# A depthwise convolution's diagonal weight tiles made in an earlier layer and kept in DRAM, and its shift divided between POOL and ACT

## The chip, the cores and the metric

One core of a Trainium2 chip. The metric is the device time of one execution in microseconds (us), lower is better. The kernel before takes 2172.09 us, the median of 3 runs (2170.27 to 2172.36).

## The reference

A decoder trunk of four layers over 512 tokens of width 1024. Every layer adds a token mixer and then an MLP (1024 to 4096 to 1024, squared ReLU) to the residual rows. Layers 0 and 3 mix by attention within a window, layer 1 by a Conformer convolution module, layer 2 by a gated linear recurrence (HGRN2). The change concerns layer 1, and layer 0's MLP as a place for its work. Cut to that:

```
def conformer_conv(h, w_pw1, b_pw1, w_dw, b_dw, ln_g, ln_b, w_pw2, b_pw2):
    u = h @ w_pw1 + b_pw1
    a, gate = jnp.split(u, 2, axis=-1)
    u = a * jax.nn.sigmoid(gate)
    up = jnp.pad(u, ((0, 0), (CONV_WIDTH - 1, 0), (0, 0)))
    c = depthwise_conv(up, w_dw) + b_dw          # width 31, causal, 1024 channels
    c = jax.nn.silu(layer_norm(c, ln_g, ln_b))
    return c @ w_pw2 + b_pw2

for i in range(DEPTH):
    h = h + mixer[i](rms_norm(h, norm_mixer[i]))
    h = h + jnp.square(jax.nn.relu(rms_norm(h, norm_mlp[i]) @ mlp_w1[i])) @ mlp_w2[i]
return rms_norm(h, final_norm)
```

## The kernel before

The residual rows stay in SBUF. Every fp32 product on TensorE (PE) is done as three passes (lines 285 to 287, in `step`) over operands split in a high and a low part. For a weight, `load` makes them: ACT casts the loaded `raw` to `wh` and VectorE (DVE) subtracts, `wl = raw - wh`, both on line 262. `prefetch` does this up to five slabs ahead of PE (`W_BUFS`). Weights are loaded by SyncE (SP); for the second MLP product, POOL adds blocks of weights by accumulating DMAs (line 217).

The order of the work comes from one clock. Every `step` of PE counts it up and calls `pump`, which goes round the generators that were given to `spawn`; a generator that yields n sleeps for n steps. So a `yield` in a generator says behind how many steps of PE its next instructions stand, and each engine then runs its own list strictly in order.

An MLP (`mlp`) has four groups of 1024 hidden columns. Each begins with a first product, `linear` over four slabs of 256 columns (10.9 us each), whose results ACT turns to `us` (lines 563, 564); then come seven products of a Strassen-like scheme, whose operands `uh` and `ul` are made from `us` on lines 557 and 558 and whose results DVE adds to the rows (line 604).

Layer 1 (`conformer`) has eight blocks of 128 channels, "channel 0" to "channel 7". The pointwise product gives for each channel a gate and then a value; `glu` fetches the two from PSUM on line 930, ACT applies the sigmoid (line 933), and DVE makes the gated value on line 939. Channels 0 to 2 are convolved on DVE by `on_dve`: 30 taps each (line 893), then the subtraction of a shift (lines 881, 904). `PACE` is the least number of steps between two taps while the pointwise product lasts.

Channels 3 to 7 are convolved on PE by `on_pe`. ACT spreads the gated value over the partitions in 16 small copies (line 912); PE multiplies it with diagonal weight tiles, four groups of 9 matmuls (line 833); ACT copies the results back, four copies a group (line 919); DVE adds the bias and subtracts the shift in one instruction (line 922). The diagonal tiles, `w` of 128 x 1088, are made by DVE from the `taps` and a small identity `i4` (line 823). `Convolution.prepare` makes the first ten of the 20 while layer 1 begins, and each group's end makes one more (`build`).

`sums(j)` squares the channel on ACT (line 863) and adds channel and square to the running sums `acc1` and `acc2`, on POOL, and on DVE for the last but one (lines 868, 869). `most` then sums these over the channels with small matmuls (line 401); the last channel's sums follow at the end and are added to them in `both` (line 954). The LayerNorm's mean and root come from `both`, and with them the second pointwise product begins. The sums over the channels and the spreading of mean and root (line 391) stand on PE's list.

## Time and profile before

| | |
|---|---|
| median of 3 runs | 2172.09 us (2170.27 to 2172.36) |
| profiled execution, its own time | 2173.08 us |
| its span | 2171.3 us |
| mean granted clock of PE | 0.992 |
| busy: PE | 2121.1 us (98%) |
| busy: DVE | 1402.4 us (65%) |
| busy: ACT | 1156.5 us (53%) |
| busy: POOL | 200.5 us (9%) |
| DMA, mean over the span | 121 GB/s |

The span is the time from the first to the last instruction that the profiler saw. PE works nearly all of it. Layer 0's MLP has its first products at 167 to 211 us and again every 83 us or so; layer 1's pointwise product and convolution take 484 to 656 us, and its second pointwise product begins at 669 us.

### The profile page before, as it was taken

What the parts mean: (1) busy time and instruction counts of PE and PEld (TensorE: products, weight loads), DVE (VectorE), ACT (ScalarE), POOL (GpSimd) and SP (SyncE); (2) the same over time, 40 slices, a digit from 0 to 9 for tenths busy, and PEclk for the clock granted to TensorE, in tenths of its full rate; (3) what the DMA queues carried; (4) which work ended last, traced back from release to release, by engine and by line L of the source; (5) the groups of instructions that cost most, each with busy time, mean ns of one, the idle gap of its engine ahead of it and who ended that gap; (6) DMA issues with size and microseconds to landing.
All of it is one profiled execution on the core that took longest, in us unless ns stands there. A gap on an engine that the chain in (4) does not pass through costs nothing.

```text
span 2171.3 us, 27234 instructions
## 1 busy us (share of the span) xinstructions
PE 2121.1 (98%) x10226; PEld 1748.1 (81%) x10226; DVE 1402.4 (65%) x2226; ACT 1156.5 (53%) x2015; POOL 200.5 (9%) x193
## 2 busy tenths in 40 slices
PE   8999999999988999999999999999999999999997
PEld 7778888888877888888788888888887878888886
DVE  6864663769986375475888874547548784637547
ACT  6855454454684445445555554534536684534534
POOL 0000110110020011011300000101100000101100
PEclk9999999999998999999999999999999999999999
DMA  5154755745214375674222226567564116557553
GB/s 152 47 155 110 181 129 152 184 68 136 69 40 136 98 184 114 168 175 88 88 62 75 78 69 179 113 164 177 118 161 88 59 50 194 120 152 188 114 125 78
DMA packets 211063, 262.56 MB, mean 121 GB/s; under 512 B 9027, under 2 KB 136003, under 8 KB 210932
## 3 DMA queue, kind: packets, MB, share of 16 engines
q1 hardware_dynamic: 175540, 191.61, 28.1%
q0 software_dynamic: 35392, 69.21, 20.1%
q8 instruction: 81, 1.33, 0.2%
q14 instruction: 50, 0.41, 0.1%
HBM read 258.69 MB, written 2.10 MB: 120 GB/s over the span
## 4 chain that ended last, share of the span: by engine, by line
PE 72%; DVE 14%; ACT 5%; DMA 5%; issue 4%; SPq 0%; DVEq 0%; ACTq 0%
PE mm L285 21%; PE mm L286 21%; PE mm L287 21%; DVE wl L262 5%; DMA raw<-in_mlp_w_dram 4%; DVE rows L604 3%; PE aux L754 2%; DVE ul L558 2%; DVE uc L893 1%; PE aux L704 1%; ACT wh L262 1%; PE aux L1068 1%; ACT uc L912 1%; PE aux L438 1%; PE aux L738 1%
## 5 line engine op out<-in xcount | busy, mean ns | idle before, releaser
L262 DVE TENSOR_TENSOR wl<-raw,wh 128x1024 fp32r<-128x1024 f32 x452 | 551.2, 1220 | 538.9 <-ACT wh L262 536.3
L262 ACT CAST wh<-raw 128x1024 fp32r<-128x1024 f32 x452 | 470.0, 1048 | 497.7 <-PE mm L286 187.9
L285 PE MATMUL mm<-x,wh 128*128 128x512 f32 x1568 | 628.9, 401 | 0.0
L286 PE MATMUL mm<-x,wh 128*128 128x512 f32 x1568 | 613.7, 391 | 0.0
L287 PE MATMUL mm<-x,wl 128*128 128x512 f32 x1568 | 613.6, 391 | 0.0
L287 PEld LDWEIGHTS mm<-x,wl 128*128 128x128 f32 x1568 | 294.6, 188 | 62.5 <-issue 1.2
L286 PEld LDWEIGHTS mm<-x,wh 128*128 128x128 f32 x1568 | 295.6, 189 | 56.6 <-issue 1.8
L285 PEld LDWEIGHTS mm<-x,wh 128*128 128x128 f32 x1568 | 295.5, 188 | 55.7 <-issue 1.1
L285 PE MATMUL mm<-wh,uh 128*128 128x512 f32 x768 | 303.1, 395 | 15.9 <-DVE rows L604 12.6
L217 POOL DMA_DIRECT2D raw<-in_mlp_w_dram x128 | 153.5, 1206 | 1773.2 <-DVE wl L262 928.4
L286 PE MATMUL mm<-wl,uh 128*128 128x512 f32 x768 | 300.0, 391 | 0.0
L287 PE MATMUL mm<-wh,ul 128*128 128x512 f32 x768 | 298.0, 391 | 0.0
L285 PEld LDWEIGHTS mm<-wh,uh 128*128 128x128 f32 x768 | 144.5, 188 | 53.8 <-issue 10.6
L287 PEld LDWEIGHTS mm<-wh,ul 128*128 128x128 f32 x768 | 144.6, 188 | 30.3
L286 PEld LDWEIGHTS mm<-wl,uh 128*128 128x128 f32 x768 | 144.8, 189 | 28.9
L563 ACT ACTIVATE relu<-mm 128x512 f32<-128x512 f32 x128 | 76.0, 594 | 166.7 <-PE mm L287 166.7
L558 DVE TENSOR_TENSOR ul<-us,uh 128x1024 fp32r<-128x1024 f32 x64 | 78.0, 1218 | 32.5 <-ACT uh L557 32.5
L604 DVE SCALAR_TENSOR_TENSOR rows<-mm,nr,rows 128x512 f32<-128x512 f32 x128 | 94.9, 741 | 0.0
L564 ACT ACTIVATE us<-relu 128x512 f32<-128x512 f32 x128 | 80.9, 632 | 3.9
L285 PE MATMUL mm<-wh,y 128*128 128x512 f32 x192 | 78.1, 407 | 1.4 <-ACT y L366 1.4
L426 ACT ACTIVATE sq<-rows 128x512 f32<-128x512 f32 x64 | 40.2, 628 | 68.3 <-DVE rows L338 54.3
L287 PE MATMUL mm<-wh,y 128*128 128x512 f32 x192 | 76.0, 399 | 0.0
(232 smaller groups left out, 2546.5 us busy)
## 6 DMA issues: line engine op xcount, KB each, us to landing
raw<-in_mlp_w_dram SPq DMA_DIRECT2D x256, 512.0 KB
raw<-in_mlp_w_dram POOLq DMA_DIRECT2D x128, 512.0 KB, 6.1
raw<-in_hgrn_w_qfig_dram SPq DMA_DIRECT2D x64, 256.0 KB
raw<-in_attn_w_qkv_dram SPq DMA_DIRECT2D x20, 512.0 KB
raw<-in_attn_w_o_dram SPq DMA_DIRECT2D x16, 512.0 KB
raw<-in_conv_w_pw_dram SPq DMA_DIRECT2D x32, 256.0 KB
raw<-in_conv_w_pw_dram SPq DMA_DIRECT2D x8, 512.0 KB
raw<-in_hgrn_w_o_dram SPq DMA_DIRECT2D x8, 512.0 KB
```

Source lines behind the costliest of these rows:

```text
L217: gp.dma_start(out=wide(to), in_=block(w, r, c, h), accum_op=ALU.add)
L262: return sc.copy(wh, raw), ve.tensor_tensor(wl, raw, wh.bitcast(F32), ALU.subtract)
L285: pe.matmul(ps, sh, mh, start=start, stop=False, skip_group_check=again)
L286: pe.matmul(ps, sh, ml, start=False, stop=False, skip_group_check=again)
L287: pe.matmul(ps, sl, mh, start=False, stop=stop, skip_group_check=again)
L426: sc.activation(scratch("sq"), rows[:, b, f * T : (f + 1) * T], AF.Square, accum_out=self.ms[:, f, b : b + 1])
L438: pe.transpose(ps[:, b * P : (b + 1) * P], rows[:, b, j * P : (j + 1) * P], ident)
L558: ve.tensor_tensor(flat[1], src, flat[0].bitcast(F32), ALU.subtract)
L563: sc.activation(s, ps, AF.Relu)
L564: sc.activation(us[j // KH][:, :, j % KH, :], s.rearrange("p (h t) -> p h t", h=2), AF.Square)
L604: ve.scalar_tensor_tensor(o, banks[bank][p], norm.r2[sign][:, b : b + 1], o, ALU.mult, ALU.add)
L754: pe.matmul(po[h * HD : (h + 1) * HD, n * P : (n + 1) * P], vtok[:, n - 1 + b, kv * HD : (kv + 1) * HD], pT[:, b, n - n0, h, :], start=b = ...
```

## The change

The diagonal tiles are no longer made in layer 1. `Convolution` is made before the layers, and `prepare` runs beside layer 0's MLP. It makes each tile in four pieces of 10, 10, 10 and 4 taps (128 x 320 and 128 x 128), 80 in all, in a buffer of two, and SP writes each to a tile in DRAM. It issues pieces only where `beside_first` is set, that is within the first product of each group. In layer 1 `build` is then one load of 544 KB by SP into the same ring of ten tiles, and `ahead` starts the first ten with seven steps between two.

Line 922 becomes two instructions: ACT adds the bias in place (line 944 of the changed kernel), POOL subtracts the shift (line 945). `PACE` goes from 2.4 to 1.8, the first shift waits 12 steps instead of 4, and `acc1` and `acc2` have places of their own.

```diff
-PACE = 2.4
+PACE = 1.8
+    beside_first = [False]
-    def mlp(i, norm, nxt):
+    def mlp(i, norm, nxt, beside=None):
+            if beside:
+                spawn(beside(mp))
+                beside_first[0] = True
                 linear(norm.xs, 4, hidden, lead=KC - 1 if g == 0 else None)
+                beside_first[0] = False
         def __init__(self):
+            dram = ctx.enter_context(tc.tile_pool(name="dram", bufs=1, space=bass.MemoryType.DRAM))
+            self.stored = [dram.tile([P, self.TAPS, 32], F32, name=f"w{n}") for n in range(4 * CONV_ON_PE)]
-        def prepare(self):
-            yield 16
+        def prepare(self, pool):
+            yield 12
...
+            piece = 10
+            for n, stored in enumerate(self.stored):
+                for x in range(0, self.TAPS, piece):
+                    while not beside_first[0]:
+                        yield 1
+                    nx = min(piece, self.TAPS - x)
+                    w = pool.tile([P, piece, 32], F32, tag="w", name="w", bufs=2)[:, :nx, :]
+                    taps = self.taps[:, n // 4, n % 4, x : x + nx]
+                    ve.tensor_tensor(
+                        w, self.i4.unsqueeze(1).broadcast_to([P, nx, 32]), taps.unsqueeze(2).broadcast_to([P, nx, 32]), ALU.mult
+                    )
+                    nc.sync.dma_start(out=stored[:, x : x + nx, :], in_=w)
+                    yield 2 + x % 20 // piece
+        def ahead(self):
             for _ in range(self.AHEAD):
+                yield 7
                 self.build()
-                yield 3
         def build(self):
-            ve.tensor_tensor(
-                w, self.i4.unsqueeze(1).broadcast_to([P, nx, 32]), self.taps[:, n // 4, n % 4, :].unsqueeze(2).broadcast_to([P, nx, 32]), ALU.mult
-            )
+            nc.sync.dma_start(out=w, in_=self.stored[n])
         def sums(j):
-                    shared[k] = tmp.tile([P, T], F32, tag="acc", name=k, bufs=2)
+                    shared[k] = cp.tile([P, T], F32, name=k)
         def first_shift():
-            yield 4
+            yield 12
         def on_pe(j, t):
-            ve.scalar_tensor_tensor(cs[j], cs[j], vec("b_dw", j), shared["shift"], ALU.add, ALU.subtract)
+            sc.activation(cs[j], cs[j], AF.Identity, bias=vec("b_dw", j))
+            gp.tensor_tensor(cs[j], cs[j], shared["shift"], ALU.subtract)
             sums(j)
...
+    conv = Convolution()
-            conv = Convolution()
-            spawn(conv.prepare())
+            conv.open()
+            spawn(conv.ahead())
-        mlp(i, mid, norm)
+        mlp(i, mid, norm, conv.prepare if i == 0 else None)
```

Three places of the engines' lists, before and in the change. The changed kernel's lines stand a little lower: 262 is 263 there, 558 is 561, 604 is 609, 863 is 885, 868 and 869 are 890 and 891, 893 is 915, 904 is 926, 912 is 934, 919 is 941, 930 is 953, 939 is 962.

DVE in layer 0's MLP, from the end of group 0's first product, before (`wl` belongs to a weight slab, `ul` to the first operands of the second product):

```order
L262 TENSOR_TENSOR wl<-raw,wh 128x1024 x5
L558 TENSOR_TENSOR ul<-us,uh 128x1024
L262 TENSOR_TENSOR wl<-raw,wh 128x1024 x4
L558 TENSOR_TENSOR ul<-us,uh 128x1024
L543 TENSOR_TENSOR us_sum<-us 128x1024
```

and the second half of the same piece in the change, from the first `ul` on:

```order
L561 TENSOR_TENSOR ul<-us,uh 128x1024
L824 TENSOR_TENSOR w<-i_145,taps 128x128
L824 TENSOR_TENSOR w<-i_145,taps 128x320 x3
L263 TENSOR_TENSOR wl<-raw,wh 128x1024
L824 TENSOR_TENSOR w<-i_145,taps 128x128
L824 TENSOR_TENSOR w<-i_145,taps 128x320
L263 TENSOR_TENSOR wl<-raw,wh 128x1024
L824 TENSOR_TENSOR w<-i_145,taps 128x320 x2
L824 TENSOR_TENSOR w<-i_145,taps 128x128
L824 TENSOR_TENSOR w<-i_145,taps 128x320 x2
L263 TENSOR_TENSOR wl<-raw,wh 128x1024
```

Two or five builds stand between two `wl`, seven in the time of a slab, and the next `ul` stands behind them. Such builds stand also ahead of this, in the output projection of layer 0's attention, and in the first products of groups 1 and 2.

DVE at the end of layer 1's pointwise product, before, from channel 1's last tap to channel 7's gated value (line 939) and on:

```order
L893 SCALAR_TENSOR_TENSOR uc<-uc,vecT 128x511
L893 SCALAR_TENSOR_TENSOR uc<-uc,vecT 128x493
L904 TENSOR_TENSOR uc<-uc,shift 128x512
L922 SCALAR_TENSOR_TENSOR uc<-uc,vecT,shift 128x512
L262 TENSOR_TENSOR wl<-raw,wh 128x1024
L930 TENSOR_TENSOR a<-mm,r_4296 128x512
L893 SCALAR_TENSOR_TENSOR uc<-uc,vecT 128x494
L939 SCALAR_TENSOR_TENSOR a<-a,vecT,gate 128x512
L893 SCALAR_TENSOR_TENSOR uc<-uc,vecT 128x495
```

and in the change, to channel 7's gated value (line 962) and on:

```order
L915 SCALAR_TENSOR_TENSOR uc<-uc,vecT 128x510
L915 SCALAR_TENSOR_TENSOR uc<-uc,vecT 128x511
L926 TENSOR_TENSOR uc<-uc,shift 128x512
L953 TENSOR_TENSOR a<-mm,r_4580 128x512
L263 TENSOR_TENSOR wl<-raw,wh 128x1024
L953 TENSOR_TENSOR a<-mm,r_4580 128x512
L962 SCALAR_TENSOR_TENSOR a<-a,vecT,gate 128x512
L263 TENSOR_TENSOR wl<-raw,wh 128x1024
L890 TENSOR_TENSOR acc_5030<-acc_5030,uc 128x512
L891 TENSOR_TENSOR acc_5031<-acc_5031,csq 128x512
```

Before, 18 taps of channel 2 (widths 494 to 511) stood behind that value; in the change all taps stand ahead of it, and only the last running sums (`acc`) behind.

ACT from channel 5's last copies back to the squares of channel 7, before (`csq` is a square, `uc<-a` the copies out, `uc<-aux` the copies back):

```order
L863 ACTIVATE csq<-uc 128x512 x2
L262 CAST wh<-raw 128x1024
L919 COPY uc<-aux 32x128
L912 COPY uc<-a 32x128 x16
L919 COPY uc<-aux 32x128 x15
L863 ACTIVATE csq<-uc 128x512
L919 COPY uc<-aux 32x128 x16
L863 ACTIVATE csq<-uc 128x512 x2
```

and in the change:

```order
L944 ACTIVATE uc<-uc,vecT 128x512
L885 ACTIVATE csq<-uc 128x512
L263 CAST wh<-raw 128x1024
L885 ACTIVATE csq<-uc 128x512
L934 COPY uc<-a 32x128 x16
L941 COPY uc<-aux 32x128 x16
L944 ACTIVATE uc<-uc,vecT 128x512
L941 COPY uc<-aux 32x128
L885 ACTIVATE csq<-uc 128x512
L941 COPY uc<-aux 32x128 x15
L944 ACTIVATE uc<-uc,vecT 128x512
L885 ACTIVATE csq<-uc 128x512
```

Each channel of PE's has a bias (line 944) ahead of its square, and between the two stands POOL's subtraction on POOL's own list. On PE, the four matmuls that sum `acc1` stood behind all 36 of channel 7; in the change they stand behind 13 of these, and those of `acc2` three further on.

## Rows read from the trace of the kernel before

**Rows 1.** Windows of 4 us; busy us and instructions, granted clock, DMA share, GB/s; sum.

```profile
652.00:656.00 4.00, 0.06 (x1) 0.10 (x1) 3.90 (x7) 2.52 (x6) 0.00 (x0) 0.92 0.71 248
...
660.00:664.00 4.00, 3.75 (x17) 3.66 (x18) 0.49 (x4) 0.00 (x1) 0.00 (x0) 0.50 1.02 387
...
sum 48.00, PE 32.62 PEld 28.71 DVE 34.47 ACT 29.86 POOL 10.39; mean PE 2.72 PEld 2.39 DVE 2.87 ACT 2.49 POOL 0.87
```

**Rows 2.** Timeline of PE: start us, us, engine, line, operation, times, [idle before].

```profile
601.30 0.39 PE L287 MATMUL mm<-x,wl 128*128 128x512 f32 x1
...
621.22 9.48 PE L833 MATMUL aux<-uc,w 128*128 128x128 f32 x72
639.67 12.04 PE L833 MATMUL aux<-uc,w 128*128 128x128 f32 x72 [8.98 <-ACT uc L919]
655.94 3.54 PE L401 MATMUL aux<-ones_d,acc 128*128 128x1 f32 x16 [4.22 <-ACT csq L863]
```

**Rows 3.** Timeline of DVE at the end of the conformer.

```profile
605.66 1.75 DVE L893 SCALAR_TENSOR_TENSOR uc<-uc,vecT 128x502 f32<-128x502 f32 x1
...
609.02 0.74 DVE L939 SCALAR_TENSOR_TENSOR a<-a,vecT,gate 128x512 f32<-128x512 f32 x1
...
610.82 0.73 DVE L893 SCALAR_TENSOR_TENSOR uc<-uc,vecT 128x504 f32<-128x504 f32 x1
...
628.14 0.68 DVE L930 TENSOR_TENSOR a<-mm,r 128x512 f32<-128x512 f32 x1
...
629.81 1.75 DVE L939 SCALAR_TENSOR_TENSOR a<-a,vecT,gate 128x512 f32<-128x512 f32 x1
...
663.41 0.16 DVE L954 TENSOR_TENSOR both<-most,aux 128x8 f32<-128x8 f32 x1 [3.73 <-PE aux L401]
```

**Rows 4.** Timeline of ACT there.

```profile
609.79 6.95 ACT L912 COPY uc<-a 32x128 f32<-32x128 f32 x16 [4.52 <-DVE a L939]
...
628.72 0.38 ACT L919 COPY uc<-aux 32x128 f32<-32x128 f32 x1
631.59 6.84 ACT L912 COPY uc<-a 32x128 f32<-32x128 f32 x16 [2.50 <-DVE a L939]
638.45 5.87 ACT L919 COPY uc<-aux 32x128 f32<-32x128 f32 x15
...
654.56 1.29 ACT L863 ACTIVATE csq<-uc 128x512 f32<-128x512 f32 x2 [1.26 <-DVE uc L904]
```

**Rows 5.** Groups of DVE's instructions, 484 to 656: busy us, mean ns, idle before.

```profile
L823 DVE TENSOR_TENSOR w<-i,taps 128x1088 f32<-128x1088 f32 x20 | 25.4, 1280 | 0.0
...
L922 DVE SCALAR_TENSOR_TENSOR uc<-uc,vecT,shift 128x512 f32<-128x512 f32 x5 | 3.7, 745 | 8.1 <-ACT uc L919 8.1
```

**Rows 6.** Windows of two stages (columns as in rows 1).

```profile
484.00:632.00 148.00, 144.83 (x775) 120.30 (x773) 139.99 (x189) 93.87 (x180) 18.32 (x13) 1.00 0.32 86
...
250.00:294.00 44.00, 44.00 (x195) 36.44 (x195) 13.15 (x12) 17.74 (x24) 2.38 (x2) 1.00 0.56 135
```

**Rows 7.** Timeline of POOL in the conformer.

```profile
604.75 2.12 POOL L868 TENSOR_TENSOR acc<-acc,uc 128x512 f32<-128x512 f32 x1 [16.91 <-DVE uc L922]
...
623.11 1.27 POOL L868 TENSOR_TENSOR acc<-acc,uc 128x512 f32<-128x512 f32 x1 [14.55 <-DVE uc L904]
```

**Rows 8.** Timeline of SP at the kernel's end: the last write.

```profile
2167.78 0.33 SPq L511 DMA_DIRECT2D out_dram<-rows  x1
```

**Rows 9.** Waits of SP's queue: total us, times, longest.

```profile
SPq L1270 <- DMA out_dram<-rows: 1.7, 1, 1.7
```

**Rows 10.** Timeline of DVE in layer 0's MLP, first product of group 0.

```profile
198.55 1.23 DVE L262 TENSOR_TENSOR wl<-raw,wh 128x1024 fp32r<-128x1024 f32 x1 [4.69 <-ACT wh L262]
...
209.43 1.23 DVE L262 TENSOR_TENSOR wl<-raw,wh 128x1024 fp32r<-128x1024 f32 x1 [6.94 <-ACT wh L262]
...
214.39 1.23 DVE L558 TENSOR_TENSOR ul<-us,uh 128x1024 fp32r<-128x1024 f32 x1 [1.02 <-ACT uh L557]
```

**Rows 11.** Timeline of PE there: the second product.

```profile
216.99 0.39 PE L287 MATMUL aux<-wh,ul 128*128 128x512 f32 x1
```

More of the change, by code (lines that the diff above doesn't have):

```diff
@@ L793, in __init__ @@
         def __init__(self):
-            cp = self.pool = tc.tile_pool(name="cv", bufs=1)
-            self.cp = cp.__enter__()
             self.built = []
-            self.taps = self.cp.tile([P, CONV_ON_PE, 4, self.TAPS], F32, name="taps")
-            self.i4 = self.cp.tile([P, 32], F32, name="i4")
-        def close(self):
-            self.pool.__exit__(None, None, None)
-        def prepare(self):
-            yield 16
+            dram = ctx.enter_context(tc.tile_pool(name="dram", bufs=1, space=bass.MemoryType.DRAM))
+            self.stored = [dram.tile([P, self.TAPS, 32], F32, name=f"w{n}") for n in range(4 * CONV_ON_PE)]
+            self.taps = const.tile([P, CONV_ON_PE, 4, self.TAPS], F32, name="taps")
+            self.i4 = const.tile([P, 32], F32, name="i4")
+        def prepare(self, pool):
+            yield 12
             j0, r0 = KC - CONV_ON_PE, vrows["w_dw"]
@@ L807, in prepare @@
             ve.memset(self.taps, 0.0)
-            yield 2
+            yield 4
             for g in range(4):
```

12 lines of the change are left out of this document (8 added, 4 removed).

## The prediction

> **What bounds the kernel now.** I read the page first: PE is busy 98% of the span (the table above), so a change on DVE, ACT or POOL can only win where PE waits for them. The table of windows says where that is. In the 48 us from 628 to 676 PE works 32.62 us [rows 1]; it does next to nothing in 652 to 656, and its granted clock stands at 0.50, the lower of its two levels (1.2 GHz), in 660 to 664. This is the end of the conformer: the depthwise convolution of its last channel block (channel 7 below), then the LayerNorm sums. Everything the change moves out of the conformer must pay here or nowhere.
>
> Next, who was late. PE ends the last product of the pointwise projection at 621.22, where its convolution of channel 6 begins [rows 2]; DVE fetches that product only at 628.14 and hands over channel 7's gated values ("a7", line 939) at 629.81 + 1.75 = 631.56 [rows 3]; ACT begins channel 7's 16 copies at 631.59 and ends the last at 638.43 [rows 4]; PE begins channel 7's convolution at 639.67, after 8.98 us of waiting [rows 2]. Channel 6 is the same: PE ends that product at 601.69 [rows 2], and a6 is handed over at 609.02 + 0.74 = 609.76 [rows 3]. So DVE runs some 7 to 8 us behind PE. But ACT is nearly as late: from 609.79 to 628.72 + 0.38 = 629.10 it works without a gap [rows 4], 19.3 us, and then waits only 2.50 for a7. This is the point on which my forecast turns.
>
> After that the chain is PE (36 matmuls, 12.04, to 651.71), ACT's last copies, DVE's shift, the squares on ACT (654.56), 16 sum matmuls, and "both" on DVE at 663.41 [rows 2, 3, 4].
>
> **The change, part by part.** The sum is made against the profiled execution, 2173.08 us; the median of the three runs, 2172.09, is 0.99 lower.
>
> *1. The conformer up to channel 7's copies.* DVE loses 20 tile builds (25.4 us) and five shifts (3.7 us) of the 139.99 us that it works in 484 to 632 [rows 5, 6]. If a7 followed directly it would come far earlier. But the order fills the room: the taps of the three channels that DVE convolves itself, which before ran on into PE's idle time (633 to 653), now all stand ahead of a7. Between the gated values of channels 4 and 5 stood 14 taps, 4 builds and a shift, and now 24 taps; between 5 and 6, 16 taps, 4 builds and a shift, and now 21 taps and a subtraction; between 6 and 7, 14 taps, 2 builds and two shifts, and now 7 taps and one. A tap is 0.73 alone [rows 3], of which some 0.65 is its step in a row of taps (0.08 overlaps the next); a build is 1.28, a step of 1.20. So: 4 to 5, 14 x 0.65 + 4.8 + 0.67 = 14.6 against 24 x 0.65 = 15.6, +1.0; 5 to 6, 15.9 against 14.3, -1.6. That is -0.6 for a6.
>
> POOL then gives some of it back. Its subtraction is of the form of the running sums it already makes, 2.12 beside a working DVE and 1.27 when DVE rests [rows 7]. The tap at 605.66 that runs beside one takes 1.75, one at 610.82 that runs alone 0.73 [rows 3]: +1.02 to DVE. Two such subtractions (of channels 3 and 4) run before a6 is made: +2.0. a6 comes at 609.76 - 0.6 + 2.0 = 611.2.
>
> From there ACT has its own list in order: channel 6's 16 copies, 16 copies back of channel 5, gate, table load, two weight casts, one bias, two squares, then channel 7's copies. It is the 19.3 us of before, less one copy (0.38), plus a bias that I take at the 0.63 of a square (two in 1.29 [rows 4]) and a wait for POOL's subtraction between bias and square, 1.27: 20.8. Channel 7's copies start at 632.0 (before 631.59): **+0.4**. a7 itself is 7 taps, two fetches, two wl and a subtraction behind a6, some 10 us, and is not what ends last. Bounds: -6.5 (rival A), and +2 with POOL's 2.12 in place of 1.27 and a third collision.
>
> *2. The tail.* Copies of channel 7 end at 632.0 + 6.84 = 638.8; the 16 copies back of channel 6 at 645.1 (15 took 5.87 [rows 4]); bias 645.8; POOL 647.1; DVE's add 647.8. PE starts at 640.2 on channel 7. Its order now holds a sum over acc1 after 13 of the 36 matmuls, and that sum waits for this add. The lower clock makes the first ones slow: 36 took 12.04 here, but 9.48 for channel 6 (0.263 each) [rows 2]; at 0.5 us each for the 11 of the first 5.4 us, the 13 end at some 646.3, so PE is held 1.5 us. Then two groups of sum matmuls, about 1.0 each at full clock (16 rows take 3.54, or 1.8 a group, at the lower one [rows 2]), and 23 x 0.263 = 6.05: 655.9. Copies back 1.6, bias 0.63, POOL 1.27, square 0.63: 660.0. Two groups of sums remain instead of four: the first at 659.4, and with 1.8 for each "both" stands at 663.1, against 663.41. So the tail is 31.1 long instead of 31.8: **-0.7**. What was gained (two sums off the end, a DVE list that is empty) is given back by three engines in a row (ACT, POOL, ACT) where one DVE instruction of 0.74 stood. Bounds: -2.4 if the hold does not occur, +5 if it costs the clock (rival D).
>
> *3. The builds in layer 0's MLP.* 80 pieces, 320 or 128 wide; by width a wide one is about 1.28 x 320/1088 + 0.05 = 0.43. The first products leave room: in 250 to 294 DVE works 13.15 of 44.00 [rows 6], and 24 or 28 builds are 12. The two-buffer tile is the question: two more builds need two writes landed. The nearest write is the kernel's last, 512 KB: 0.33 of issue, then 1.7 of waiting [rows 8, 9], 2.0 in all. A pair of 160 KB pieces thus comes round in 0.43 + 2.0 + 0.33 for the second issue = 2.8. Seven builds stand in each slab of 10.88 us (the step between the wl rows, 198.55 to 209.43 [rows 10]), which allows 3.1 a pair. **0**, with little to spare; other end in rival B. ACT and PE see nothing of it while wl and ul keep their places: ul is made at 214.39 + 1.23 = 215.62 and first used at 216.99 [rows 10, 11], 1.4 of slack.
>
> *4. The rest.* 16 builds in attention 0's output projection, PE saturated there: **0**, at most +1. Twenty reads of 544 KB on SP: 11.1 MB at 387 GB/s [rows 1] are 29 us of DMA time in a stretch of 148 us that uses 0.32 of it [rows 6]: **0**, at most +3 should one of the loads queue behind a read that waits for its write. The changed pace and the copies of taps are in the orders above.
>
> Sum: 2173.08 + 0.4 - 0.7 = 2172.8, as a median **2171.8**: no change.
>
> **A rule against the change.** Row first: beside a POOL operation of 2.12 the tap grew by 1.02, not by 2.12 [rows 3, 7]. The Trainium skill, "SBUF — State Buffer", section "Who interferes with whom", says that a VectorE instruction with two SBUF inputs and a GpSimd instruction that reads SBUF exclude each other: whoever is first holds the shared ports for its whole instruction. By it moving a subtraction to POOL can take all of POOL's time from DVE. This trace agrees that the two collide, not that one is blocked throughout.
>
> **Rivals.**
> A, *DVE was the only late engine* (faster). Without builds DVE keeps up and fetches each product when PE ends it: a6 at 601.69 + 0.68 + 0.74, and a wl (1.21) in the way, 604.3; ACT's 20.8 gives 625.1, 6.5 before 631.59. With the tail, 2173.08 - 6.5 - 0.7 = 2165.9, median 2164.9. For it: 29 us really leave DVE, and it is DVE that ended ACT's waits. Against it: the order puts 24 and 21 taps where builds stood. 0.25.
> B, *DVE waits for the writes* (slower). If a pair's writes queue behind the loads of the same slab (135 GB/s [rows 6] x 10.88 us is 2.9 loads of 512 KB, each 1.35 us at 387 GB/s, for 3.5 pairs), a pair takes 2.8 + 0.83 x 1.35 = 3.9. It decides from 3.1 on. Over the last 13 builds ahead of ul the delay is 6.5 x 0.8 - 1.4 = 3.8, in two groups 7.6: median 2179.4. For it: the margin is 0.3 us. Against: the row of 2.0 is for three times the bytes. 0.15.
> C, *POOL holds DVE throughout*: 1.77 for 1.02 at the two subtractions ahead of a6, +1.5: 2173.3, still no change. The Trainium skill's rule named above would make it so. 0.06.
> D, *the hold keeps PE at 1.2 GHz* (slower). The 23 matmuls at 0.5 are 5.4 longer than at 0.263: median 2177.2. For it: the clock did fall after waits here [rows 1]. 0.09.
>
> **How the numbers follow.** Forecast 0.45, its own range 2168 to 2176.5 (-4 and +4.5, the bounds of parts 1, 2 and 4 together); A 0.25, B 0.15, C 0.06, D 0.09. The limit of 0.2% is 4.3 us, about what a measurement of this kernel can tell from no change: 2167.7 and 2176.4. Faster: A and 0.03 of the forecast, 0.28. Slower: B, D and 0.03, 0.27. The same: 0.45. The range takes in A and B: 2163.5 to 2180.
>
> **What would show it.** Right: ACT's copies of channel 7 start at 631 to 633 with no wait for DVE before them; the sum over acc1 begins 1 to 2 us after the matmul before it; "both" at about 663; no wait of DVE for a write in 165 to 300 that delays a wl. Wrong: copies of channel 7 at 627 or earlier (A); PE idle before a product with ul in layer 0's MLP, the conformer shifted later as a whole (B); a granted clock of 0.50 from the hold to the end of channel 7 (D).

## The result: 1.1% slower, lost in layer 0

| | before | after |
|---|---|---|
| median | 2171.64 us (4 runs, 2170.27 to 2172.36) | 2196.44 us (4 runs, 2193.01 to 2198.63) |
| ratio | | 1.0114, 95% interval 1.0096 to 1.0131 |
| span of the profiled execution | 2171.3 us | 2196.9 us |
| busy: PE, DVE, ACT, POOL | 2121.1, 1402.4, 1156.5, 200.5 | 2130.1, 1406.4, 1160.0, 206.7 |
| written to HBM | 2.10 MB | 13.24 MB |

24.8 us more, where no change was forecast (2171.8, range 2163.5 to 2180.0). The side is that of rival B, the size more than three times its price.

**Where the time went.** PE does the same 8160 weight matmuls in the same order in both. So the n-th of them in one trace can be set against the n-th in the other: its start after, less its start before. I give that "lateness" for eight places; the second row says where the matmul stands in the trace of before. The runs of the experiments are in the same table, since each of them is read from it (in seven of them some of the 8160 change places with near ones, 132 at most).

| matmul n | 336 | 480 | 672 | 1056 | 1152 | 2064 | 2304 | last |
|---|---|---|---|---|---|---|---|---|
| at, before | 142 | 178 | 222 | 311 | 333 | 547 | 682 | 2163 |
| stage | layer 0: attention, end | MLP, group 0, first product | after its first ul | group 1, after its first ul | group 1 | layer 1: pointwise product | its second one | |
| after | 2.4 | 8.5 | 13.2 | 21.7 | 20.7 | 21.7 | 23.8 | 25.4 |
| no_write | 3.7 | 3.7 | 3.7 | 2.9 | 2.6 | 2.3 | 6.0 | 3.1 |
| write_free | 2.8 | 6.6 | 6.6 | 6.0 | 6.1 | 6.4 | 8.5 | 8.4 |
| no_build | 2.8 | 2.8 | 2.8 | 2.0 | 1.8 | 1.3 | 3.7 | -0.5 |
| write_act | 2.1 | 11.3 | 17.3 | 32.3 | 31.3 | 31.7 | 35.4 | 35.1 |
| nb_late | 1.6 | 1.8 | 1.8 | 4.3 | 5.9 | 11.2 | 16.6 | 11.5 |
| spread_held | 2.0 | 2.1 | 2.1 | 9.1 | 16.6 | 26.7 | 28.7 | 29.9 |
| nb_keep | 2.7 | 2.7 | 2.7 | 1.8 | 1.5 | 2.0 | -2.4 | -4.9 |
| bufs5 | 3.1 | 6.7 | 16.1 | 15.3 | 15.3 | 15.6 | 19.2 | 20.1 |
| bufs5_keep | 1.3 | 6.1 | 15.6 | 14.1 | 14.1 | 14.4 | 7.8 | 6.9 |
| before_split | -0.3 | -0.3 | -0.3 | -0.9 | -1.1 | -1.0 | -3.0 | -2.6 |
| bk22 | -1.4 | -1.4 | -1.4 | -2.2 | -2.2 | -2.4 | 1.5 | -0.8 |
| bks22 | -0.7 | -0.7 | -0.7 | -1.5 | -1.7 | -1.6 | 0.5 | -0.1 |
| paced | 0.3 | 0.3 | 4.8 | 4.3 | 4.3 | 4.8 | 10.2 | 8.2 |
| paced_keep | 0.8 | 0.8 | 5.3 | 4.4 | 4.5 | 4.8 | -1.4 | -0.6 |
| nb_keep20 | 2.4 | 2.4 | 2.4 | 1.5 | 1.1 | 0.7 | -5.4 | -8.9 |
| paced_keep_dve | -0.2 | -0.2 | 2.4 | 3.1 | 3.6 | 4.0 | -0.3 | -1.9 |
| paced_keep_g0 | 0.6 | 0.6 | 0.7 | 1.8 | 3.1 | 6.4 | -0.3 | -1.9 |
| paced_keep_b5 | 0.5 | 0.5 | 0.5 | 0.0 | 0.0 | -0.1 | -5.8 | -4.6 |

A difference along a row is time won or lost there; one trace against another leaves about 1 us of the start. The late layers, which no edit touches, wander by up to 5 between the last two columns (no_build from 3.7 to -0.5, nb_late from 16.6 to 11.5), so the last column is no measure of an edit.

The row "after" says it at once: 2.4 in attention 0, then 6.1, 4.7 and 8.5 at three places of layer 0's MLP, 2.1 at the end of layer 1, and small change. What DVE did there, in the timeline of the changed kernel (start, length, engine, line, tile, times, and in brackets the idle time before the row and what ended it):

```profile
167.43 0.49 DVE L824 TENSOR_TENSOR w<-i,taps 128x320 f32<-128x320 f32 x1 [3.76 <-DMA w<-w]
170.50 0.29 DVE L824 TENSOR_TENSOR w<-i,taps 128x128 f32<-128x128 f32 x1 [2.57 <-DMA w<-w]
...
173.78 0.68 DVE L339 TENSOR_TENSOR rows<-rows,mm 128x512 f32<-128x512 f32 x1
...
180.21 0.69 DVE L824 TENSOR_TENSOR w<-i,taps 128x320 f32<-128x320 f32 x2 [2.22 <-DMA w<-w]
180.82 2.72 DVE L448 SCALAR_TENSOR_TENSOR x<-aux,vecT,x 128x512 fp32r<-128x512 f32 x4
...
219.24 0.49 DVE L824 TENSOR_TENSOR w<-i,taps 128x320 f32<-128x320 f32 x1 [3.79 <-DMA w<-w]
221.52 0.89 DVE L824 TENSOR_TENSOR w<-i,taps 128x128 f32<-128x128 f32 x2 [1.79 <-DMA w<-w]
...
226.03 1.22 DVE L263 TENSOR_TENSOR wl<-raw,wh 128x1024 fp32r<-128x1024 f32 x1
227.17 1.22 DVE L561 TENSOR_TENSOR ul<-us,uh 128x1024 fp32r<-128x1024 f32 x1
```

It waits for "DMA w<-w", the write of a piece two builds earlier, up to 4.4 us at a time (the table below). Behind the waits stands what PE needs next: `rows` (line 339) at 173.78, the last sum of attention 0's output projection, and at 227.17 the `ul` (line 561) with which PE's second product of group 0 begins. In [rows 10] that `ul` began at 214.39; the sum of `rows`, line 338 there, stood in the kernel before at

```profile
166.79 0.68 DVE L338 TENSOR_TENSOR rows<-rows,mm 128x512 f32<-128x512 f32 x1
```

The totals, by the table of waits (total us, times, longest):

```profile
DVE w L824 <- DMA w<-w: 73.8, 39, 4.4
```

```profile
PE aux L855 <- ACT uc L941: 10.4, 2, 9.9
PE aux L288 <- DVE ul L561: 9.3, 2, 6.6
...
PE aux L439 <- DVE rows L339: 3.8, 1, 3.8
PE aux L402 <- POOL uc L945: 3.7, 1, 3.7
```

So the first of the three losses is not in the MLP's own builds: PE waits 3.80 for `rows` at the start of the MLP, behind the builds that stand in attention 0's output projection, and only 0.2 for `x` (line 448, at 180.82). The other two are the two `ul`, 9.3 us together.

```profile
174.52 0.47 PE L439 MATMUL aux<-ident,rows 128*128 128x128 f32 x1 [3.80 <-DVE rows L339]
...
319.20 0.80 PE L288 MATMUL aux<-wh,ul 128*128 128x512 f32 x1 [6.56 <-DVE ul L561]
```

PE pays once more when it goes on: after the 6.56 its granted clock is at the lower level for a while (the table of windows, columns as in [rows 1]), and from 326 it is 1.00 again. After the 3.80 it was 0.80 and 0.77 in 172 to 180.

```profile
318.00:322.00 4.00, 2.80 (x7) 2.23 (x8) 4.00 (x6) 1.05 (x1) 1.19 (x1) 0.50 0.84 215
322.00:326.00 4.00, 4.00 (x14) 3.16 (x13) 3.40 (x5) 1.48 (x2) 1.20 (x1) 0.68 0.89 131
```

Layer 1 went much as the prediction had it up to channel 7's copies. ACT, DVE, POOL and PE there:

```profile
633.40 6.95 ACT L934 COPY uc<-a 32x128 f32<-32x128 f32 x16 [2.99 <-DVE a L962]
...
652.21 0.63 ACT L885 ACTIVATE csq<-uc 128x512 f32<-128x512 f32 x1 [1.44 <-POOL uc L945]
...
654.21 6.79 ACT L934 COPY uc<-a 32x128 f32<-32x128 f32 x16
661.01 6.21 ACT L941 COPY uc<-aux 32x128 f32<-32x128 f32 x16
```

```profile
632.63 0.74 DVE L962 SCALAR_TENSOR_TENSOR a<-a,vecT,gate 128x512 f32<-128x512 f32 x1
...
648.43 1.23 DVE L263 TENSOR_TENSOR wl<-raw,wh 128x1024 fp32r<-128x1024 f32 x1 [7.24 <-ACT wh L263]
...
650.29 0.75 DVE L962 SCALAR_TENSOR_TENSOR a<-a,vecT,gate 128x512 f32<-128x512 f32 x1
...
669.35 0.69 DVE L890 TENSOR_TENSOR acc<-acc,uc 128x512 f32<-128x512 f32 x1 [13.41 <-POOL uc L945]
...
686.86 0.16 DVE L977 TENSOR_TENSOR both<-most,aux 128x8 f32<-128x8 f32 x1 [13.88 <-PE aux L402]
```

```profile
662.60 6.85 PE L855 MATMUL aux<-uc,w 128*128 128x128 f32 x26 [9.94 <-ACT uc L941]
670.19 1.02 PE L402 MATMUL aux<-ones_d,acc 128*128 128x1 f32 x8 [0.75 <-DVE acc L890]
...
672.64 6.90 PE L855 MATMUL aux<-uc,w 128*128 128x122 f32 x40
683.25 1.87 PE L402 MATMUL aux<-ones_d,uc 128*128 128x1 f32 x8 [3.71 <-POOL uc L945]
```

Less the 21.74 by which layer 1 starts late, a6 is made at 611.6 (632.63 + 0.74) and channel 7's copies start at 632.5; a7 has been ready for three us by then (650.29 + 0.75 = 651.04 against 654.21) and ACT works without a wait for DVE between 633.40 and 654.21. The matching rows of before are [rows 3, 4].

### The profile page after: what moved, and what is told of

The parts are those of the page before. It is cut to its first block, busy times and chain, and to the rows that moved or that the text cites. A ratio compares the mean times of both kernels' runs of the same rounds, so it can differ in the third digit from the quotient of the medians.

```text
span 2196.9 us, 27550 instructions
## 1 busy us (share of the span) xinstructions
PE 2130.1 (97%) x10226; PEld 1751.6 (80%) x10226; DVE 1406.4 (64%) x2281; ACT 1160.0 (53%) x2020; POOL 206.7 (9%) x198
## 3 DMA queue, kind: packets, MB, share of 16 engines
q8 instruction: 81, 1.33, 0.2%
HBM read 269.83 MB, written 13.24 MB: 129 GB/s over the span
## 4 chain that ended last, share of the span: by engine, by line
PE 62%; DVE 16%; DMA 10%; issue 8%; ACT 4%; POOL 0%; SPq 0%; DVEq 0%; ACTq 0%; POOLq 0%
PE mm L286 18%; PE mm L287 17%; PE mm L288 17%; DVE wl L263 6%; DMA w<-w 5%; DMA raw<-in_mlp_w_dram 4%; DVE rows L609 3%; DVE ul L561 2%; PE aux L759 2%; PE aux L709 1%; DVE uc L915 1%; ACT wh L263 1%; PE aux L1091 1%; PE aux L439 1%; PE aux L743 1%
## 5 line engine op out<-in xcount | busy, mean ns | idle before, releaser
L824 DVE TENSOR_TENSOR w<-i,taps 128x320 f32<-128x320 f32 x80 | 33.8, 440 | 75.6 <-DMA w<-w 73.8
L286 PE MATMUL mm<-wh,y 128*128 128x512 f32 x192 | 78.2, 407 | 1.4 <-ACT y L367 1.4
```

Source lines behind the costliest of these rows:

```text
L286: pe.matmul(ps, sh, mh, start=start, stop=False, skip_group_check=again)
L824: ve.tensor_tensor(w, self.i4.unsqueeze(1).broadcast_to([P, nx, 32]), taps.unsqueeze(2).broadcast_to([P, nx, 32]), ALU.mult)
```

## The experiments

All are built on the changed kernel unless said otherwise. The kernel before ran beside them, at medians of 2169.4 to 2171.5; each ratio is to the runs beside it, and a difference of two runs that had different runs of before beside them is safer by the ratios.

**1. Builds without writes.**

```diff
-                    nc.sync.dma_start(out=stored[:, x : x + nx, :], in_=w)
-            nc.sync.dma_start(out=w, in_=self.stored[n])
+            nc.sync.dma_start(out=w, in_=mlp_w1[1][n % 8 * P : n % 8 * P + P, : self.TAPS * 32].rearrange(...))
```

> The 80 builds stay in DVE's list in layer 0, but they are not written to DRAM (the loads in layer 1 take other data of the same size), so no build waits for a write. Theory (the loss in layer 0's MLP, 18.3 us between the first slab of its first group and group 2, is DVE waiting for the writes of the two-buffer tile with wl, x and ul queued behind): that loss goes, and the kernel takes 2196.4 - 18.3 = about 2178, with no wait of DVE for a DMA of w. Rival 1 (the builds' own 28 us of DVE work delay wl and ul): it stays near 2196. Rival 2 (the 11 MB of writes slow the weight loads): about 2178 too, and told apart by write_free.

2173.68 us, 1.001 (1.0001 to 1.0019). The loss in layer 0's MLP is gone (3.7 from attention 0 on, and no more up to group 1). Rival 1 falls: the builds' own work costs nothing where it now stands. That is not where it stood: with no write to wait for, all 80 builds are done by 190, 44 of them before 170, while the change builds until 378. Run 13 has builds in all four groups.

**2. Writes that no build waits for.**

```diff
-                    nc.sync.dma_start(out=stored[:, x : x + nx, :], in_=w)
+                    nc.sync.dma_start(out=stored[:, x : x + nx, :], in_=self.taps.rearrange(...)[:, : 32 * nx].rearrange(...))
```

> The 80 builds and the 80 writes both stay, of the same sizes and in the same places, but each write takes its data from the table of taps instead of the tile just built, so that no build waits for a write; what is stored is not the tile. Theory (waiting): about 2178, as without writes, within 2 us. Rival 2 (DMA traffic of the writes, which share the 16 engines with the weight loads): stays at 2190 or more. In between, by so much as the traffic counts.

2182.12 us, 1.0049 (1.0034 to 1.0065). In between: 14.3 less than the change, and 8.4 over no_write, so about two thirds of the loss is waiting and the rest goes with the writes as such. In the trace 3.8 of the 8.4 fall at one place, the start of group 0, where a `wl` ahead of `x` waits for a weight that landed late; against no_write, 2.8 more come behind layer 1 (the last two columns), in layers that no edit touches, and I can't say why. The expectation was wrong in one point: the builds, as in 1, are not in the same places. Without a buffer to wait for, DVE's list has up to 17 of them in a row (5.92 us from 187.07 on), which by itself costs nothing. The split of the loss holds for writes bunched like this (timeline of write_free):

```profile
175.86 1.23 DVE L263 TENSOR_TENSOR wl<-raw,wh 128x1024 fp32r<-128x1024 f32 x1 [3.88 <-ACT wh L263]
177.00 2.72 DVE L448 SCALAR_TENSOR_TENSOR x<-aux,vecT,x 128x512 fp32r<-128x512 f32 x4
```

**3. Neither builds nor writes.**

```diff
+            return
             piece = 10
```

(and the loads as in 1)

> Neither builds nor writes in layer 0, only the 16 copies of taps; the loads in layer 1 take other data of the same size. What is left is the change in layer 1 alone. Theory: 2196.4 - 18.3 for the MLP and up to 2.4 for attention 0, so 2175.7 to 2178, that is 4 to 6 slower than the kernel before, of which 2 are the end of the conformer (both sums 1.7 later against the start of layer 1 than before) and the rest drift and layer 0's start. Rival (the conformer gains when layer 0 leaves it alone, since DMA and DVE start it undisturbed): below 2171.

2173.89 us, 1.001 (1.0001 to 1.0019): the builds are free, and the change in layer 1 with the copies of taps is 2.4 slower than before. The table has 2.8 by the end of attention 0 and 2.4 more at the end of layer 1. The first is in DVE's list: 8 and 4 copies (line 814) stand ahead of three `wl` at 40.78, which before began at 38.10, and PE waits for the last of them and for what follows (timelines of no_build).

```profile
36.68 2.07 DVE L814 COPY taps<-vecT 32x155 f32<-32x155 f32 x8
...
40.78 3.50 DVE L263 TENSOR_TENSOR wl<-raw,wh 128x1024 fp32r<-128x1024 f32 x3
```

```profile
42.06 0.50 PE L288 MATMUL mm<-x,wl 128*128 128x512 f32 x1 [0.54 <-DVE wl L263]
...
45.14 0.35 PE L709 MATMUL aux<-kh,qs 128*128 128x256 f32 x1 [1.19 <-DVE qs L693]
```

**4. The shift alone, in the kernel before.**

```diff
-            ve.scalar_tensor_tensor(cs[j], cs[j], vec("b_dw", j), shared["shift"], ALU.add, ALU.subtract)
+            sc.activation(cs[j], cs[j], AF.Identity, bias=vec("b_dw", j))
+            gp.tensor_tensor(cs[j], cs[j], shared["shift"], ALU.subtract)
```

> The kernel before, with line 922 alone made into a bias on ACT and a subtraction on POOL. Theory (ACT and POOL in a row cost more at the end than DVE's one instruction, and nothing is won before it since ACT is as late as DVE): the tail +1.2 (0.72 + 1.27 for 0.74), and channel 7's copies 0 to 2 later: 2172 to 2175. Rival (DVE is the late engine, and 3.7 us less work there bring channel 7 forward): 2168 to 2170.

2170.17 us, 0.9994 (0.9986 to 1.0003): no difference that can be told in the time; the trace has 2.0 won at the end of layer 1. That is the rival's direction, but not its path: channel 7's copies start at 633.81, later than the 631.59 before, as the theory had it. What is won lies behind them: "both" stands at 660.53, before at 663.41, so the tail that the theory made 1.2 longer is shorter. In the kernel before, the shift of channel 6 on DVE waits for ACT and holds nine taps behind it; in before_split twelve taps run on without a wait.

```profile
644.35 0.75 DVE L922 SCALAR_TENSOR_TENSOR uc<-uc,vecT,shift 128x512 f32<-128x512 f32 x1 [4.71 <-ACT uc L919]
645.02 8.78 DVE L893 SCALAR_TENSOR_TENSOR uc<-uc,vecT 128x503 f32<-128x503 f32 x9
```

```profile
635.48 9.32 DVE L893 SCALAR_TENSOR_TENSOR uc<-uc,vecT 128x500 f32<-128x500 f32 x12
```

**5. The writes issued by ACT.**

```diff
-                    nc.sync.dma_start(out=stored[:, x : x + nx, :], in_=w)
+                    nc.scalar.dma_start(out=stored[:, x : x + nx, :], in_=w)
```

> The changed kernel with the 80 writes issued by ACT instead of SP; builds, buffers and order of DVE's builds as in the change. Theory (a write waits behind the weight loads that SP has issued before it on the same 16 DMA engines, whoever issues it): the time from issue to the build that reuses the buffer stays at some 4 us (median 3.8 in the change) and the kernel at 2190 to 2198, or worse, since ACT's own list now holds issues that wait for builds. Rival (SP's own queue is the cause: its list or its ring is served in order): from issue to reuse falls to about 2, as in the quiet cases (1.6 to 1.9), and the kernel to 2182 or less.

2206.39 us, 1.0163 (1.015 to 1.0177). From a write's issue to the build that takes its buffer again the median is 3.7 us, against 3.8 in the change: SP's queue is not the cause. ACT now waits for builds, which is worse (the table of waits; the results' `relu` waits 17.4 more):

```profile
ACT wh L263 <- DVE w L824: 17.6, 7, 4.8
```

**6, 7. Copies and builds held back in the program's order.** `keep` (line 80) makes an instruction keep the program's order against others that are kept. Here it is put on the weight subtractions of layer 0 and on the copies (nb_late), and on the builds too, with no gate and `yield 5` (spread_held).

```diff
+        if held[0]:
+            keep(sub)
-            yield 12
+            while not beside_first[0]:
+                yield 1
+                    keep(ve.tensor_copy(...))
```

> As no_build (no builds and writes in layer 0, the loads in layer 1 take other data), but the 16 copies of taps are held until the first product of layer 0's MLP; to hold them, DVE's list keeps the program's order between them and the weight subtractions of layer 0. Theory (12 of these copies, 3.4 us, stood on DVE ahead of three weight subtractions in layer 0's attention, at 36.7 to 40.8, and PE came 2 to 2.4 later from there on): 2.0 to 2.4 less than no_build, 2171 to 2172, and a start of layer 0's MLP as in the kernel before. Rival (these 2 are given back within the attention): the same as no_build, 2173.9.

> The whole change again, with builds and writes, but the copies of taps as in nb_late, and the builds spread over all of layer 0's MLP, one in five steps (3.4 us), held in the program's order against the weight subtractions. Two buffers as before, so a pair has 6.8 us for its writes instead of 3.1. Theory: the waits (14.3 of the loss, change against write_free) and the copies (2.4) go, the traffic of the writes stays (8.4 or less): 2179.6, not under 2173.9. Rival (builds between the second products, where DVE is busy 33 of 39 us, delay operands): over 2185.

2184.81 us (1.0062, 1.005 to 1.0075) and 2201.41 us (1.0138, 1.0123 to 1.0154). Both missed. The copies do leave the attention (1.6 there instead of 2.8), but nb_late, which has no builds, loses some 9 us in layer 0's MLP: with the weight subtractions kept to the program's order DVE's list is worse than without. PE now waits for `wl` there (5.7 us in 150 to 560), and not once in the kernel before. So neither run speaks to its question; another way to move builds was needed (11 to 15).

**8. The gated values kept ahead of the taps**, on 3, with `PACE = 2.4`:

```diff
-            ve.scalar_tensor_tensor(u, t, vec("b_pw1", j, 0), gates[j], ALU.add, ALU.mult)
+            ins = ve.scalar_tensor_tensor(u, t, vec("b_pw1", j, 0), gates[j], ALU.add, ALU.mult)
+            if j >= ON_DVE:
+                keep(ins)
-                    ve.scalar_tensor_tensor(c[:, late:], ...)
+                    ins = ve.scalar_tensor_tensor(c[:, late:], ...)
+                    if len(us) > ON_DVE:
+                        keep(ins)
```

> As no_build, but the gated values of the channels that PE convolves keep their place in the program's order against the taps (pace 2.4): 27 taps now stand behind channel 7's value instead of none. Theory of the prediction's rival A, put to the test (DVE's taps ahead of a6 and a7 are what kept the conformer from gaining; 31 us less work on DVE then show): channel 7's copies start 4 to 7 earlier against the start of layer 1, and the kernel takes 2167 to 2170. Rival (ACT's own list of 20.8 us between channel 6's copies and channel 7's ends last, with POOL's subtraction in it): at most 2 less than no_build, 2172 to 2174.

2167.64 us, 0.9982 (0.9974 to 0.9991), 6.2 less than no_build. Channel 7's copies now start at 625.29, the time of rival A (625.1; layer 1 itself starts 1 to 2 late here). a6 is made at 603.6 (602.69 + 0.90), 8 us earlier than in the change, and ACT's list from there takes the same 20.7 (604.55 to 625.29). What ends last is now the 26 taps behind: PE waits 10.0 for DVE's running sums (timelines of nb_keep):

```profile
604.55 6.92 ACT L937 COPY uc<-a 32x128 f32<-32x128 f32 x16
...
625.29 6.93 ACT L937 COPY uc<-a 32x128 f32<-32x128 f32 x16
```

```profile
602.69 0.90 DVE L965 SCALAR_TENSOR_TENSOR a<-a,vecT,gate 128x512 f32<-128x512 f32 x1
...
628.12 23.61 DVE L916 SCALAR_TENSOR_TENSOR uc<-uc,vecT 128x486 f32<-128x486 f32 x26
```

**9, 10. Five buffers instead of two**, one buffer of summed weights less; bufs5_keep with 8 added, at a pace of 2.0.

```diff
-                group[key] = raw_tile(sumpool[0], bufs=8)
+                group[key] = raw_tile(sumpool[0], bufs=7 if n_layer[0] == 0 else 8)
-                    w = pool.tile([P, piece, 32], F32, tag="w", name="w", bufs=2)[:, :nx, :]
+                    w = pool.tile([P, piece, 32], F32, tag="w", name="w", bufs=5)[:, :nx, :]
```

> The whole change, with five buffers for the built pieces instead of two; the room comes from one of the eight buffers for summed weights in layer 0. Nothing else is changed. Theory (two buffers against a time of some 4 us from a write's issue to the reuse): five buffers at one build in 1.55 us allow 7 us, the builds no longer wait (their 74 us of waiting for a DMA of w fall under 10), and what stays is the traffic and the copies of taps: 2182 like write_free, within 3. Rival (the order of the builds in DVE's list, not the number of buffers): over 2190.

> As bufs5, and with the gated values of PE's channels kept ahead of the taps as in nb_keep, at a pace of 2.0 that leaves 15 taps behind channel 7's value. Theory (the two parts add up): bufs5 less the 6.2 that nb_keep gained over no_build, and up to 4 more since in nb_keep the 26 taps behind ended last (651.8, four us after ACT's copies): bufs5 less 6 to 10, about 2174. Rival (with the writes there the conformer starts with its loads of w behind, and keeps nothing): as bufs5.

2191.37 us (1.0101, 1.0086 to 1.0116) and 2181.91 us (1.0062, 1.0048 to 1.0076). The theory fell short: group 1 loses nothing now, but group 0 loses more at its `ul` (9.4), and the MLP's start still 3.6. By the ratios five buffers gain 2.8 over the change, and the two intervals overlap. The five buffers were filled at once. In DVE's list builds are drawn forward as far as buffers allow, it seems as if a write took no time, so ten pieces stand between two `wl` (timeline of bufs5) and the same wait is back:

```profile
202.88 1.93 DVE L825 TENSOR_TENSOR w<-i,taps 128x320 f32<-128x320 f32 x5 [1.13 <-DMA w<-w]
209.40 1.93 DVE L825 TENSOR_TENSOR w<-i,taps 128x320 f32<-128x320 f32 x5 [4.58 <-DMA w<-w]
211.24 1.22 DVE L264 TENSOR_TENSOR wl<-raw,wh 128x1024 fp32r<-128x1024 f32 x1
```

The conformer's part of bufs5_keep is as expected: 6.6 won between the two pointwise products (14.4 to 7.8), and 9.5 less than bufs5.

**11, 12. The kernel before with the gated values kept ahead**, at a pace of 2.2, as it is (bk22) and with the split shift (bks22).

> The kernel before, builds in layer 1 and shift on DVE as they were, with nothing but the gated values of PE's channels kept in the program's order against the taps (pace 2.2 instead of 2.4). Theory (the order of the taps, not the builds, decides when channel 7's copies start): 2 to 5 less than before, 2166 to 2169. Rival (with the builds on DVE it has no room, and what is taken off ahead of channel 7 comes last behind it): 2171 or more.

> As bk22, with the shift divided between ACT and POOL as in the change. Theory: before_split gained 1.3 in the median over the kernel before, since DVE is the engine with the longest list there; on top of bk22 another 0 to 2: 2164 to 2168, below both kernels. Rival (ACT's list of 20.8 between channels 6 and 7 ends last once the taps are out of the way, and the bias and the wait for POOL lengthen it): 1 to 2 above bk22.

2173.06 us (1.0019, 1.001 to 1.0028) and 2173.93 us (1.0024, 1.0014 to 1.0034). Both missed. With the builds on DVE, channel 7's copies start no earlier against layer 1's own start (629.25 + 2.4 in bk22, 633.64 + 1.6 in bks22, before 631.59), and the taps that are taken off ahead of channel 7 come last behind it: PE waits for DVE's running sums, 7.2 and 3.3. As far as these two runs at one pace show, moving the builds is needed for the gain, as the change meant it.

**13. Builds paced by a true dependence.** Two buffers, as in the change.

```diff
+                    if beside:
+                        zero = mp.tile([P, 1], F32, tag="zero", name="zero", bufs=2)
+                        sc.mul(zero, s[:, :1], 0.0)
+                        zeros.append(zero)
...
+            flat = self.taps.rearrange("p a b c -> p (a b c)")
+            ve.tensor_scalar(flat, flat, zeros[0], None, ALU.add)
...
+                i4 = pool.tile([P, 32], F32, tag="i4e", name="i4e", bufs=1)
+                ve.tensor_scalar(i4, self.i4, zeros[e], None, ALU.add)
+                for _ in range((3, 2)[e % 2]):
```

> The whole change with two buffers, but the builds and the copies of taps get a true dependence on the first product's results: after each 128-column result ACT makes a zero from it, DVE adds it to the small identity, and the next three or two builds use that. So at most three builds stand between two weight subtractions (five in 10.9 us instead of seven, over all four groups), and none nor the copies of taps in layer 0's attention. Theory (the list packs builds ahead of wl, x and ul, since it is made without the time of the writes; two buffers then hold up what stands behind): the waits and the attention's 2 us go, the writes' traffic stays: 2171 + 8.4 at most + conformer 2.5, so 2174 to 2180, and five buffers are not needed. Rival (a build that waits stalls PE wherever it stands): over 2185.

2178.88 us, 1.0039 (1.0026 to 1.0051). The same 80 builds and writes with the same two buffers, 17.6 less than the change (16 by the ratios): where and how densely they stand decides. The run doesn't tell apart the bounded packing, the lower rate, the four groups instead of three and the empty attention. Attention 0 loses nothing, and in layer 0's MLP one place is left, `ul` of group 0 (4.5). But the end of layer 1 loses 5.4, where the change lost 2.1 with the same code: PE's hold at `acc1` was 1.86 here, the clock behind it the lower one, and channel 7's last 20 matmuls took 7.98 (columns as in [rows 1]).

```profile
656.00:660.00 4.00, 4.00 (x19) 3.54 (x18) 0.17 (x1) 0.83 (x3) 0.00 (x0) 0.50 0.00 0
660.00:664.00 4.00, 4.00 (x19) 3.68 (x18) 0.00 (x0) 1.21 (x4) 0.00 (x0) 0.55 0.00 0
```

**14. The same with 8.**

> As paced, with the gated values of PE's channels kept ahead of the taps (pace 2.0, 15 taps behind channel 7's value). Theory: the conformer gains 6.0 against the start of layer 1, as bufs5_keep showed, instead of losing 2.5: paced less 8 or 9, 2166 to 2172, at or below the kernel before. Rival: the writes' traffic takes it all, 2174 or more.

2170.79 us, 1.0003 (0.9994 to 1.0011): level with the kernel before; 4.5 lost in layer 0, 6.2 won at the end of layer 1.

**15. The bound: 8 at a pace of 2.0, without builds.**

> As nb_keep (no builds and no writes in layer 0, other data loaded in layer 1), at a pace of 2.0, which leaves 15 taps instead of 27 behind channel 7's value. It bounds what the conformer's part can give when layer 0 costs nothing. Theory: in nb_keep the taps behind ended last, some 4 us after ACT's copies, so 2 to 4 below it: 2164 to 2166. Rival (more taps ahead hold channels 6 and 7 up by as much): the same as nb_keep, 2167.6.

2162.56 us, 0.9965 (0.9951 to 0.9978), 5.1 under nb_keep (4.0 when each is set against before beside it). This leaves out the builds; it is what layer 1 gives with these lists.

**16. Bias and shift on DVE again, on 14.**

> As paced_keep, with bias and shift again one instruction on DVE. Theory (with DVE relieved, ACT's list between channels 6 and 7 ends last; the bias and the wait for POOL's subtraction are 2 us of it, and the tail's three engines in a row another 1.2): 1 to 3 below paced_keep. Rival (DVE's instruction waits in its list behind taps): the same or above.

2172.52 us, 1.0007 (0.9999 to 1.0016): not below 14, and the two intervals overlap. The split earns a little or nothing here as well.

**17, 18. The place that is left.** On 14: no builds at group 0's last two results and more later (paced_keep_g0), or five buffers as in 9 (paced_keep_b5).

> As paced_keep, with no builds at the last two results of group 0 and three instead of two at some results of the later groups. In paced_keep the one loss left in layer 0 was 4.5 us at ul of group 0, where the last three builds of that group stood just ahead of it behind a wait of 5.1 for a write. Theory: that goes, and the kernel takes 2170.8 - 4.5 = 2166 to 2167, below the kernel before. Rival (three builds at a result bring the same wait to the later groups): 2169 or more.

> As paced_keep, with five buffers for the pieces (one buffer for summed weights less in layer 0). With the packing bounded, buffers should now do what they did not do in bufs5: no build waits for a write ahead of ul. Theory: the loss at ul of group 0 goes, 2166 to 2167, and the builds' waits for w fall from 37 us to under 10. Rival (the loss is the traffic, weights that come late, and no matter of buffers): 2170 or more.

2171.21 us (1.0005, 0.9996 to 1.0014) and **2166.82 us (0.9984, 0.9975 to 0.9993)**. Moving three builds only moved the wait: the later groups now lose 5.7 together (0.7 to 6.4). Five buffers with bounded packing remove it. Up to layer 1 this kernel is within 0.5 of before everywhere, with 80 builds and 11 MB of writes in it, and no wait of DVE for a write is left (the table of waits of paced_keep_b5, 160 to 480; `i4e` are the waits for ACT's zeros):

```profile
DVE i4e L831 <- ACT zero L572: 47.4, 14, 4.5
DVE wl L265 <- ACT wh L265: 45.4, 39, 3.9
```

So up to layer 1 the writes' traffic costs nothing that shows when they are spread over four groups; bunched, in write_free, it cost some 4 in layer 0. Against 15, which has neither builds nor writes, this kernel is level at the second pointwise product (-5.8 and -5.4) and yet 4.3 slower in all; these 4 fall in later layers, where PE waits 11.1 for `rows` and 7.3 in 15, and no run here says why. This kernel beats both: the one before by 3.4, the change by some 28 (by the ratios).

## Why the prediction was wrong, point by point

- **The step that failed: part 3**, "a pair of 160 KB pieces thus comes round in 0.43 + 2.0 + 0.33", 2.8, within the 3.1 that the list allows. The 2.0 of the kernel's last write holds where little else moves. In the change a write takes from its issue to the reuse of its buffer 3.8 us in the median. The 18 shortest took 1.6 to 2.1, with a DMA share of 0.14 to 0.49 meanwhile; of the 33 that took 3.8 to 7.4 all but one had 0.60 or more. The write that I took [rows 8, 9] had no load beside it; the stretch to be priced has a DMA share of 0.56 [rows 6]. The term was 0 and measured 18.3 (2.4 to 20.7 in the table), in it 6.1 that began in part 4's output projection.
- **Rival B** had the mechanism, at 3.9 a pair and 7.6 in all. It priced the delay at the `ul` of two groups, 3.8 each, and there 4.7 and 9.4 were lost. It missed the place before: the builds that stand in attention 0's output projection (part 4: "PE saturated there: **0**, at most +1") wait for their writes too, and the last sum of `rows` stands behind them. PE waited 3.80 for it, and with the clock behind the wait 6.1 were lost by the first product. And it left out the clock after each wait.
- **Part 4, copies of taps.** I wrote that they were "in the orders above" and gave them no price. Twelve of them stand ahead of three `wl` in attention 0: 2 to 2.4 us, shown by no_build (2.8 by then) against paced (0.3). The twenty reads cost nothing that shows, as forecast: no_build has loads of the same size, and its lateness falls from 1.8 to 1.3 up to matmul 2064.
- **Part 1 was right in time and mechanism:** a6 at 611.2, measured 611.6; channel 7's copies at 632.0, measured 632.5, with ACT's list ending last. One piece was off without harm: a7 came 17.7 behind a6 instead of some 10, since a `wl` ahead of it waited 7.24 for a cast in that same list of ACT (648.43). It was right that the order, not the work, decides: nb_keep and nb_keep20, with the taps behind, start the copies at 625.3 and 624.1. Rival A's 7.2 is what nb_keep20 wins against before (7.4); nb_keep wins 3.4. POOL's subtraction took 1.33 there (1.27 taken).
- **Part 2 was 2.0 off:** "both" at 663.1 forecast, 686.86 - 21.74 = 665.1 measured. PE ended channel 7 at 679.54 - 21.74 = 657.8 instead of 655.9. The hold at acc1 was 0.75 instead of 1.5, but the 23 matmuls behind it took 7.8 instead of 6.05, the 20 last of them 6.90: 0.35 each, between the price at the one clock and at the other, at a granted clock of 0.59 in 672 to 676 and 0.98 in 676 to 680. So a part of rival D happened here, and most of it in paced (13). The last two sums then cost what was forecast.
- **Rival C and the ports.** I read [rows 3, 7] wrongly in the prediction: there is blocking throughout. In the change the tap at 627.59 starts while POOL subtracts and ends at 629.36, 0.55 after POOL's end (628.81). The next one, at 629.39, ends at 631.04, 0.55 after POOL's add (630.49). It goes the other way too: the subtraction ends 1.14 after the `wl` that was running (627.67), and the add 1.13 after the first tap. [Rows 3, 7] have the same: the tap at 605.66 ends 0.54 after POOL's 604.75 + 2.12, and all nine of DVE's taps, weight subtractions and gated values that start beside such a sum in the kernel before end 0.53 to 0.55 after it. So each engine waited in turn until the other's whole instruction was done. The Trainium skill, "SBUF — State Buffer", section "Who interferes with whom", calls the ports that the two share an exclusive lock. This trace agrees. The two taps so met lost 2.06 together (3.45 where two alone took 1.39), 1.03 each: the 1.02 of the prediction and not rival C's 1.77, because a long row of POOL begins with POOL's own wait for DVE. So rival C had the mechanism and a price too high; the +2.0 of part 1 was right, its reason was not.

```profile
626.45 1.22 DVE L263 TENSOR_TENSOR wl<-raw,wh 128x1024 fp32r<-128x1024 f32 x1
627.59 1.77 DVE L915 SCALAR_TENSOR_TENSOR uc<-uc,vecT 128x502 f32<-128x502 f32 x1
629.39 1.65 DVE L915 SCALAR_TENSOR_TENSOR uc<-uc,vecT 128x503 f32<-128x503 f32 x1
```

```profile
626.83 1.98 POOL L945 TENSOR_TENSOR uc<-uc,shift 128x512 f32<-128x512 f32 x1 [1.61 <-ACT uc L944]
628.89 1.60 POOL L890 TENSOR_TENSOR acc<-acc,uc 128x512 f32<-128x512 f32 x1
...
650.85 1.33 POOL L945 TENSOR_TENSOR uc<-uc,shift 128x512 f32<-128x512 f32 x1 [18.68 <-ACT uc L944]
```

## What to carry to other kernels

A transfer's time must be read in the stretch where it will run, with its loads; here the row from the kernel's quiet end (2.0) was near the shortest of them (1.6), and the median was 3.8. When work is moved into an engine's idle time, ask what paces it: idle time that is filled up front, with a wait in it, delays all that stands behind, and the fix here was a dependence that spreads the pieces, then buffers, in that order. And work that leaves a busy engine pays only if the order lets the late instruction move up: here removing 29 us from DVE gave nothing until the gated values were kept ahead of the taps.

## What the runs showed that I had not expected

- More buffers alone gave 5.1 (bufs5; 2.8 by the ratios), since the list grew with them: ten builds between two `wl` in place of five. Two buffers with bounded packing and a lower rate gave 17.6 (16).
- A wait of PE in the middle of the MLP costs more than itself: after 6.56 us of it the granted clock was 0.50 and 0.68 in the next two windows of 4 us, and the place lost 9.4 (12.35 to 21.7 between matmuls 768 and 1056).
- DVE and POOL shut each other out for whole instructions, and the loss on DVE was still only 1.0 per meeting: it is what is left of POOL's instruction that counts, not its row's length.
